# 64 tokens instead of 32 beside the gathered tile: 320 dense columns, rows from the queries on, row operands in PSUM, every second low part on GpSimd

## The chip, the core and the metric

One core of a Trainium2 chip runs the whole kernel. Its engines are TensorE (PE, matrix products into PSUM), VectorE (DVE), ScalarE (ACT), GpSimd (POOL, which also issues the gathers) and SyncE (SP, which issues the loads). The metric is the device time of one execution in microseconds.

## The reference

One layer on 512 tokens of width 2048, in float32: a mixer of two attentions, then a product-key expert layer, then a last RMSNorm. The change touches the expert layer alone:

```
def peer_ffn(h, w_query, sub_keys, expert_u, expert_v):
    q = (ht @ w_query).astype(jnp.float32).reshape(n_tok, PEER_HEADS, 2, HALF_KEY)
    scores = jnp.einsum('thpc,hpnc->thpn', q, sub_keys.astype(jnp.float32))
    s1, i1 = lax.top_k(scores[:, :, 0], PEER_TOPK)
    s2, i2 = lax.top_k(scores[:, :, 1], PEER_TOPK)
    ...
    top_score, pos = lax.top_k(cand_score, PEER_TOPK)
    expert_ids = jnp.take_along_axis(cand_id, pos, axis=-1)
    gates = jax.nn.softmax(top_score, axis=-1)
    ...
        u_sel = expert_u[idb]
        act = jax.nn.gelu(jnp.einsum('thkd,td->thk', u_sel, xb).astype(jnp.float32))
        w = (gb * act).astype(xb.dtype)
        v_sel = expert_v[idb]
        return jnp.einsum('thk,thkd->td', w, v_sel)
```

Each token picks 16 experts in each of 8 heads, 128 of 16384; an expert is one row of `expert_u` and one of `expert_v`, of 2048 numbers (8 KB) each.

## The kernel before

Activations lie with the feature dimension on partitions (`acc`: 16 tiles of 128 x 512 tokens). A product in float32 is made of three matmuls (`mm3`): `wload` loads a weight tile in two halves of 128 x 1024, ACT rounds each half to `wh` (the high part) and DVE subtracts to get `wl` (the low part); PE then multiplies wh by the two parts of the activation and wl by its high part. One `wload` feeds 48 matmuls. `wh` and `wl` have three buffers each, and the raw tiles four in all.

The expert layer is computed in two ways at once. For the first `TD` = 352 tokens (the dense ones) all 16384 experts are computed: `expert_up(c)` makes the activations of 128 experts with one wload of `uT` into the PSUM tile `psu`, and the products with `vP` go by groups of `GC` = 8 such chunks into `psy`, 16 output tiles to a group, each added to `acc` by DVE. The gates, zero for experts not chosen, are scattered through DRAM (`gsp`) and multiplied into the activations (`weigh`). The first `NS` = 54 activations are made before the gates are known and wait in DRAM (`gact_sp`, written and fetched again).

For the last 160 tokens the chosen rows are fetched. POOL issues an indirect DMA that brings 128 rows, one to each partition (`row_of`, a tile `row` of 128 x 2048). The last 128 tokens take one partition each and need 128 fetches from `expert_u` and 128 from `expert_v`. The `MB` = 32 tokens before them lie four times on the partitions (`GB` = 4 groups), so 32 fetches of each table (`SB`) serve them. For a row of `expert_u` one DVE operation multiplies it by the token's features `h2g` and sums up; for one of `expert_v` another adds it, times its weight, to the result. After the last one `back` and `back_b` transpose the results into `acc`.

The rows stand in a list `todo`. Each place in the code that calls `pace(ins, units)` adds `units * rate` to a counter; for each whole number reached, the next entry of the list is issued, its DVE work tied to come after `ins`. `rate` is `SLOW` = 0.8 until the down-projections begin, and then what spreads the rest evenly up to eight wloads before the end. Row buffers: two, and a third from the down-projections on. All engines run their instructions in the order that the framework's scheduler set.

Stages: attention and output projection; the queries (`psq2`, 16 wloads of `w_q`, per head the DVE chain `choose` for the gathered tokens); the choice for the dense tokens, woven with 40 early up-projections; the scatter of the gates with 14 more (`psgt`, `ab`); the down-projections, first with activations from DRAM, then alternating with the 74 up-projections that are left; the last norm.

Of the kernel before, what the change touches and what calls it, by code (L numbers as in the profile page):

```python
# [35 lines left out]
MB = 32  # L36
# [8 lines left out]
SLOW = 0.8  # L45
# [5 lines left out]
def block_kernel(ctx, tc, xT, gains, w_vf, bf, w_qk, w_v, w_g, w_br, w_o, w_q, keysT, uT, vP, expert_u, expert_v, outT):  # L51
# [43 lines left out]
    def wload(src, between=None, pace=None):  # L95
# [3 lines left out]
        for s in range(2):  # L99
# [9 lines left out]
            ins = nc.vector.tensor_tensor(lo, raw, hi.bitcast(F32), op=ALU.subtract)  # L109
            out.append((hi, lo))  # L110
            if pace and s == 0:
                pace(ins, 0.5)
# [378 lines left out]
    py = pool("py", 2, space=PSUM)  # L491
    gpool = pool("gath", 1)
    h2g = gpool.tile([P, KC, P], F32, name="h2g")
# [8 lines left out]
    rows_p = pool("rows", 1)  # L502
    accg = acc[:, :, T - P:]
    def norm2():
        ps = py.tile([P, T], F32, tag="py", name="psn2")
        nc.tensor.matmul(ps, ones, rstd, start=True, stop=True)
        rsqrt(rstd, ps, [gl.tile([P, T], F32, tag="gl", name="rs2") for i in range(3)])
        pt = py.tile([P, NT, P], F32, tag="py", name="psrt")
# [5 lines left out]
    def token_rows(cols, dst, x_dst=None):  # L514

        for j in range(0, KC, 4):
            if x_dst is not None:
                ps = py.tile([P, 4, P], F32, tag="py", name="psxg")
                for i in range(4):
                    nc.tensor.transpose(ps[:, i], cols(j + i), ident)  # L520
            ph = py.tile([P, 4, P], F32, tag="py", name="pshg")
            for i in range(4):
                tmp = gl.tile([P, P], F32, tag="gl", name="tmp")
                src = cols(j + i)
                nc.vector.tensor_scalar(tmp if len(src.shape) == 2 else tmp.rearrange("p (g m) -> p g m", m=MB), src,
                                        g_sb[:, KC + j + i:KC + j + i + 1], None, op0=ALU.mult)
# [19 lines left out]
    accb = h2g  # L546
    count, extra = [0], []
# [9 lines left out]
    def row_of(table, ids, i):  # L557
        count[0] += 1
        third = extra and count[0] % 3 == 0
        row = (extra[0] if third else rows_p).tile([P, KC, P], F32, tag="row", bufs=1 if third else 2, name="row")  # L560
# [4 lines left out]
    def gather_up(i, after):  # L565
        row = row_of(expert_u, idx, i)
        with tc.issue_after(after):
            nc.vector.scalar_tensor_tensor(row, row, rstd_t[:, NT - 1:NT], h2g, op0=ALU.mult, op1=ALU.mult,  # L568
                                           accum_out=gact[:, i:i + 1])

    def rows_b(i, after):
        token_rows(lambda k: acc[:, k, TD:TD + MB].unsqueeze(1).to_broadcast([P, GB, MB]), h2g)

    def gather_up_b(i, after):
        row = row_of(expert_u, idx_b, i)
        with tc.issue_after(after):
            nc.vector.scalar_tensor_tensor(row, row, rstd_b, h2g, op0=ALU.mult, op1=ALU.mult,
                                           accum_out=gact_b[:, i:i + 1])

    def gather_down(i, after):  # L580
# [3 lines left out]
        row = row_of(expert_v, idx, i)  # L584
        with tc.issue_after(after):
            nc.vector.scalar_tensor_tensor(accg, row, gact[:, i:i + 1], accg, op0=ALU.mult, op1=ALU.add)  # L586

    def gather_down_b(i, after):
# [3 lines left out]
        row = row_of(expert_v, idx_b, i)  # L592
        with tc.issue_after(after):
            if i == 0:
                nc.vector.tensor_scalar(accb, row, gact_b[:, :1], None, op0=ALU.mult)
            else:
                nc.vector.scalar_tensor_tensor(accb, row, gact_b[:, i:i + 1], accb, op0=ALU.mult, op1=ALU.add)

    def back(i, after):
        for j in range(0, KC, 4):  # L600
            ps = py.tile([P, 4, P], F32, tag="py", name="psback")
            for i in range(4):
                nc.tensor.transpose(ps[:, i], accg[:, j + i], ident)
            nc.scalar.activation(accg[:, j:j + 4], ps, AF.Copy)

    def back_b(i, after):
        for j in range(0, KC, 4):
            ps = py.tile([P, 4, MB], F32, tag="py", name="psbackb")
            for i in range(4):
                nc.tensor.matmul(ps[:, i], accb[:, j + i], sel_b, start=True, stop=True)  # L610
# [4 lines left out]
    todo += [(gather_down_b, i) for i in range(SB)] + [(lambda i, after: None, 0), (back, 0), (back_b, 0)]  # L615
    rate = [SLOW]

# [10 lines left out]
    with ExitStack() as s1:  # L628
# [3 lines left out]
        psx = pool("psx", 2, space=PSUM, cm=s1)  # L632
        pg = pool("pg", 2, space=PSUM, cm=s1)
# [82 lines left out]

        for h in range(NH):
            sc = []
            sv = se.tile([P, 2, HT, NK], F32, tag="sv", name="sv")
            for p in range(2):  # L720
# [3 lines left out]
                if b == 3:  # L724
                    token_rows(lambda k: acc[:, k, T - P:], h2g, accg)
                ps = pu.tile([P, T], F32, tag="pu", name="psq2")
                proj(ps, wload(w_q[b]), h2)
# [4 lines left out]
                ps = psx.tile([P, NT, NK], F32, tag="psx", name="pss")  # L732
# [16 lines left out]
        ps = psx.tile([P, T], F32, tag="psx", name="psrep")  # L749
# [177 lines left out]
```

## Time and profile before

| | |
|---|---|
| time, median of 3 runs | 3787.84 us (3779.3 to 3790.0) |
| the profiled execution, its own time | 3782.03 us |
| its span, first to last instruction | 3780.3 us |
| PE, DVE, ACT, POOL busy | 97%, 70%, 34%, 14% |
| DMA | 827.26 MB, mean 219 GB/s |
| mean granted PE clock | 0.989 |

Busy shares are means over all stages. A matmul's record overlaps the next one's, so what one matmul costs is read from the distance of two starts, not from its own length.

### The profile page before, as it was taken

What the parts mean: (1) busy time and instruction counts of PE and PEld (TensorE: products, weight loads), DVE (VectorE), ACT (ScalarE), POOL (GpSimd) and SP (SyncE); (2) the same over time, 40 slices, a digit from 0 to 9 for tenths busy, and PEclk for the clock granted to TensorE, in tenths of its full rate; (3) what the DMA queues carried; (4) which work ended last, traced back from release to release, by engine and by line L of the source; (5) the groups of instructions that cost most, each with busy time, mean ns of one, the idle gap of its engine ahead of it and who ended that gap; (6) DMA issues with size and microseconds to landing.
All of it is one profiled execution on the core that took longest, in us unless ns stands there. A gap on an engine that the chain in (4) does not pass through costs nothing.

```text
span 3780.3 us, 52236 instructions
## 1 busy us (share of the span) xinstructions
PE 3676.0 (97%) x20745; PEld 3384.4 (90%) x20745; DVE 2640.2 (70%) x4067; ACT 1291.3 (34%) x1808; POOL 515.2 (14%) x432
## 2 busy tenths in 40 slices
PE   8999999999999999999999898999999999999997
PEld 7888888888887878799999798999999999999997
DVE  5333445444555346799699888988888888888885
ACT  4334222232223223344355332333333333333333
POOL 0000000000000000011211122222222222222220
PEclk9999999999999999999999999999999999999999
DMA  4222222222224233376867899998999989999983
GB/s 141 80 78 77 98 95 95 89 87 84 85 95 138 95 100 101 128 267 251 294 229 264 288 336 333 352 334 326 333 336 348 345 324 349 340 343 344 332 306 112
DMA packets 233701, 827.26 MB, mean 219 GB/s; under 512 B 21736, under 2 KB 82664, under 8 KB 189680
## 3 DMA queue, kind: packets, MB, share of 16 engines
q1 hardware_dynamic: 174032, 450.30, 34.5%
q0 software_dynamic: 49920, 360.74, 24.8%
q10 hardware_dynamic: 9504, 12.88, 0.9%
q8 instruction: 163, 2.67, 0.3%
q14 instruction: 82, 0.67, 0.1%
HBM read 784.72 MB, written 39.11 MB: 218 GB/s over the span
## 4 chain that ended last, share of the span: by engine, by line
PE 81%; DVE 9%; DMA 5%; issue 3%; ACT 1%; SPq 0%; POOL 0%; DVEq 0%; POOLq 0%; ACTq 0%
PE psy L118 7%; PE psy L117 7%; PE psy L116 7%; PE psu L118 6%; PE psu L116 6%; PE psu L117 6%; PE psg L118 3%; PE psg L117 3%; PE psq L118 3%; PE psg L116 3%; PE psq L117 3%; PE psq L116 3%; DVE wl L109 2%; DVE ab L787 2%; PE psk L118 2%
## 5 line engine op out<-in xcount | busy, mean ns | idle before, releaser
L108 ACT ACTIVATE wh<-wr 128x1024 fp32r<-128x1024 f32 x768 | 813.6, 1061 | 1933.4 <-PE psy L117 581.0
L109 DVE TENSOR_TENSOR wl<-wr,wh 128x1024 fp32r<-128x1024 f32 x768 | 935.5, 1221 | 504.4 <-ACT wh L108 500.5
L116 PE MATMUL psy<-wg,wh 128*128 128x352 f32 x2048 | 668.6, 327 | 26.6 <-ACT wg L820 25.8
L117 PE MATMUL psy<-wg,wh 128*128 128x352 f32 x2048 | 672.0, 328 | 8.7 <-DVE wg L821 8.7
L118 PE MATMUL psu<-h,wl 128*128 128x352 f32 x2048 | 666.7, 326 | 12.8 <-DVE wl L109 12.5
L118 PE MATMUL psy<-wg,wl 128*128 128x352 f32 x2048 | 669.8, 328 | 8.4 <-DVE wl L109 8.3
L116 PE MATMUL psu<-h,wh 128*128 128x352 f32 x2048 | 666.6, 325 | 4.0 <-DVE gl L536 2.9
L117 PE MATMUL psu<-h,wh 128*128 128x352 f32 x2048 | 662.8, 324 | 0.0
L116 PEld LDWEIGHTS psy<-wg,wh 128*128 128x128 f32 x2048 | 391.1, 191 | 29.0 <-ACT wg L820 27.6
L118 PEld LDWEIGHTS psu<-h,wl 128*128 128x128 f32 x2048 | 385.5, 188 | 18.9 <-DVE wl L109 18.7
L117 PEld LDWEIGHTS psy<-wg,wh 128*128 128x128 f32 x2048 | 391.0, 191 | 11.0 <-DVE wg L821 10.9
L118 PEld LDWEIGHTS psy<-wg,wl 128*128 128x128 f32 x2048 | 391.0, 191 | 10.0 <-DVE wl L109 9.9
L116 PEld LDWEIGHTS psu<-h,wh 128*128 128x128 f32 x2048 | 386.6, 189 | 5.0 <-issue 3.2
L117 PEld LDWEIGHTS psu<-h,wh 128*128 128x128 f32 x2048 | 386.9, 189 | 0.0
L561 POOL DMA_INDIRECT row<-eu,idx x128 | 192.4, 1503 | 901.5 <-DVE row L568 606.4
L568 DVE SCALAR_TENSOR_TENSOR row<-row,rstd_t,h2g 128x2048 f32<-128x2048 f32 x128 | 300.1, 2345 | 6.5 <-DMA row<-eu,idx 6.5
L586 DVE SCALAR_TENSOR_TENSOR acc<-row,gact,acc 128x2048 f32<-128x2048 f32 x128 | 300.1, 2345 | 1.9 <-DMA row<-ev,idx 1.9
L561 POOL DMA_INDIRECT row<-ev,idx x128 | 182.2, 1424 | 508.0 <-DVE acc L586 478.1
L116 PE MATMUL psq<-h,wh 128*128 128x512 f32 x512 | 204.5, 399 | 8.8 <-ACT wh L108 8.8
L117 PE MATMUL psq<-h,wh 128*128 128x512 f32 x512 | 205.6, 401 | 1.5 <-DVE h L167 1.4
L118 PE MATMUL psq<-h,wl 128*128 128x512 f32 x512 | 204.6, 400 | 0.1
L118 PE MATMUL psg<-h,wl 128*128 128x512 f32 x512 | 203.3, 397 | 0.0
(311 smaller groups left out, 5513.7 us busy)
## 6 DMA issues: line engine op xcount, KB each, us to landing
wr<-uT SPq DMA_DIRECT2D x256, 512.0 KB
wr<-vP SPq DMA_DIRECT2D x256, 512.0 KB
wr<-w_qk SPq DMA_DIRECT2D x64, 512.0 KB
wr<-w_g SPq DMA_DIRECT2D x64, 512.0 KB
gsp<-st POOLq DMA_DIRECT2D x22, 1024.0 KB
wr<-w_br SPq DMA_DIRECT2D x32, 512.0 KB
wr<-w_o SPq DMA_DIRECT2D x32, 512.0 KB
wr<-w_q SPq DMA_DIRECT2D x32, 512.0 KB
```

The lines of the kernel that those rows point to most:

```text
L108: nc.scalar.activation(hi, raw, AF.Copy)
L109: ins = nc.vector.tensor_tensor(lo, raw, hi.bitcast(F32), op=ALU.subtract)
L116: nc.tensor.matmul(ps, wh, ah, start=start, stop=False)
L117: nc.tensor.matmul(ps, wh, al, start=False, stop=False)
L118: nc.tensor.matmul(ps, wl, ah, start=False, stop=stop)
L561: nc.gpsimd.indirect_dma_start(out=row.rearrange("p k q -> p (k q)"), out_offset=None, in_=table, in_offset=bass.IndirectOffsetOnAxis(ap=i ...
L568: nc.vector.scalar_tensor_tensor(row, row, rstd_t[:, NT - 1:NT], h2g, op0=ALU.mult, op1=ALU.mult, accum_out=gact[:, i:i + 1])
L586: nc.vector.scalar_tensor_tensor(accg, row, gact[:, i:i + 1], accg, op0=ALU.mult, op1=ALU.add)
L787: nc.vector.tensor_scalar(ab[0][:, i], i128, tr[0][:, t:t + 1], tr[2][:, t:t + 1], op0=ALU.is_equal, op1=ALU.mult)
```

## The change

- `MB` goes from 32 to 64: 192 tokens are gathered, in the 128 of the full tile and two groups of 64 (`GB` = 2), with `SB` = 64 fetches of each table for the latter; 320 tokens stay dense, and 53 up-projections come early.
- Gathers of the full tile start in the queries' stage: after each head its part of `idx` is computed, and `qpace` takes rows that are known (`QROWS` = 0.75 times 2 units a wload, from the sixth wload on). `SLOW` becomes 1.1.
- The features that the rows are multiplied by, and the sums of the down rows, lie in PSUM (`hold`, four banks) instead of SBUF; the sums are copied to SBUF once (`sums`) before they are transposed. `back` comes right after the last row of the full tile and adds to `acc`. There are three row buffers throughout. The other PSUM pools shrink to two banks for `psu` and two shared by everything else (`px`, also `psy`, which had four).
- From the queries on, the second half's low part in each wload is computed on POOL, not on DVE.
- The gates of the next group are fetched while the present one is multiplied (`gates`), and its first activation is weighed two wloads before the group ends.

```diff
-MB = 32
+MB = 64
...
-SLOW = 0.8
+SLOW = 1.1
+QROWS = 0.75
...
-            ins = nc.vector.tensor_tensor(lo, raw, hi.bitcast(F32), op=ALU.subtract)
+            second = more and s == 1
+            ins = (nc.gpsimd if second else nc.vector).tensor_tensor(lo, raw, hi.bitcast(F32), op=ALU.subtract)
...
-    py = pool("py", 2, space=PSUM)
+    px = pool("px", 2, space=PSUM)
+    pr = pool("pr", 1, space=PSUM)
...
-    rows_p = pool("rows", 1)
-    accg = acc[:, :, T - P:]
+    rows_p = pool("rows", 3)
+    held = [None]
+
+    def hold(name):
+
+        held[0] = pr.tile([P, KC, P], F32, tag="pr", name=name)
+        return held[0]
...
-            nc.vector.scalar_tensor_tensor(row, row, rstd_t[:, NT - 1:NT], h2g, op0=ALU.mult, op1=ALU.mult,
+            nc.vector.scalar_tensor_tensor(row, row, rstd_t[:, NT - 1:NT], held[0], op0=ALU.mult, op1=ALU.mult,
                                            accum_out=gact[:, i:i + 1])
...
+    def add_row(row, g, i, ins):
+        with tc.issue_after(ins):
+            if i == 0:
+                nc.vector.tensor_scalar(hold("accg"), row, g[:, :1], None, op0=ALU.mult)
+            else:
+                nc.vector.scalar_tensor_tensor(held[0], row, g[:, i:i + 1], held[0], op0=ALU.mult, op1=ALU.add)
...
+        def qpace(after, units):
+
+            if HK - len([f for f, _ in todo if f is gather_up]) < known[0]:
+                pace(after, units)
...
-                proj(ps, wload(w_q[b]), h2)
+                proj(ps, wload(w_q[b], pace=qpace if b > 4 else None, units=2.0), h2)
...
+            nc.vector.scalar_tensor_tensor(idx[:, hk], ia[:, NT - 1, hk], float(NK), ib[:, NT - 1, hk], op0=ALU.mult,
+                                           op1=ALU.add)
+            known[0] += TOPK
...
             w = wload(vP[grp, jb])
+            if grp + 1 < NG and jb == 1:
+                gates(grp + 1)
+            if grp + 1 < NG and jb == KC // JJ - 2:
+                first.append(weigh((grp + 1) * GC))
             for jj in range(JJ):
                 j = jb * JJ + jj
-                ps = (py, py2)[j % 2].tile([P, T], F32, tag="py", name="psy")
+                ps = px.tile([P, T], F32, tag="px", name="psy")
```

How the order on two engines changes shows in three places. On POOL, all of the `expert_v` fetches for the full tile follow each other in the kernel before (`row` is the fetched tile, `ev` the table):

```order
L561 DMA row<-eu,idx 128x2048 x83
L561 DMA row<-eu,idx_b 128x2048 x32
L561 DMA row<-ev,idx 128x2048 x128
L561 DMA row<-ev,idx_b 128x2048 x32
L874 TENSOR_TENSOR acc<-acc,rstd 128x512 x4
```

In the changed kernel, in the middle of the `expert_v` fetches, low parts stand between them:

```order
L558 DMA row<-ev,idx 128x2048 x2
L111 TENSOR_TENSOR wl<-wr,wh 128x1024
L558 DMA row<-ev,idx 128x2048
L111 TENSOR_TENSOR wl<-wr,wh 128x1024
L558 DMA row<-ev,idx 128x2048 x2
L111 TENSOR_TENSOR wl<-wr,wh 128x1024
```

One or two fetches now stand behind each low part, and each low part behind the fetches before it.

On DVE, at the start of a block of up-projections in the late part, the kernel before has (`gl<-psu,rstd` takes a finished product, `gl<-gl,h_8494` multiplies by the gates):

```order
L536 TENSOR_TENSOR gl<-psu,rstd 128x352
L586 SCALAR_TENSOR_TENSOR acc<-row,gact,acc 128x16x128
L817 TENSOR_TENSOR gl<-gl,h_8494 128x352
L586 SCALAR_TENSOR_TENSOR acc<-row,gact,acc 128x16x128
L821 TENSOR_TENSOR wg<-gl,wg 128x352
L109 TENSOR_TENSOR wl<-wr,wh 128x1024 x2
```

and the changed one, near the end of the rows:

```order
L537 TENSOR_TENSOR gl<-psu,rstd 128x320
L582 SCALAR_TENSOR_TENSOR accg<-row,gact_b,accg 128x2048
L830 TENSOR_TENSOR gl<-gl,h_8494 128x320
L582 SCALAR_TENSOR_TENSOR accg<-row,gact_b,accg 128x2048
L834 TENSOR_TENSOR wg<-gl,wg 128x320
L111 TENSOR_TENSOR wl<-wr,wh 128x1024
```

One low part of the two has gone to POOL, the 352 columns are 320, and the sum `accg` is the tile in PSUM.

On DVE in the queries' stage, between the instructions of `choose`, the changed kernel has row operations, which the kernel before has only after that stage:

```order
L648 MAX v<-pss 128x8
L565 SCALAR_TENSOR_TENSOR row,gact<-row,rstd_t,h2g 128x2048
L649 MAX_INDEX i<-v,pss 128x8
L650 MATCH_REPLACE tk<-v,pss 128x128
L648 MAX v<-pss 128x8
L651 MAX v<-tk 128x8
L649 MAX_INDEX i<-v,pss 128x8
L652 MAX_INDEX i<-v,tk 128x8
L650 MATCH_REPLACE tk<-v,pss 128x128
L565 SCALAR_TENSOR_TENSOR row,gact<-row,rstd_t,h2g 128x2048
```

Sixteen of the 384 row operations stand in this stage, and about 75 before the down-projections begin (43 of 320 in the kernel before).

## Rows read from the trace of the kernel before

**Rows 1.** The page: engines' busy time; DMA share in 40 slices, in tenths.

```profile
PE 3676.0 (97%) x20745; PEld 3384.4 (90%) x20745; DVE 2640.2 (70%) x4067; ACT 1291.3 (34%) x1808; POOL 515.2 (14%) x432
...
DMA  4222222222224233376867899998999989999983
```

**Rows 2.** Windows by stage: length; PE, PEld, DVE, ACT, POOL busy; clock; DMA share, GB/s.

```profile
1372.00:1590.00 218.00, 214.40 (x1006) 174.25 (x1007) 151.15 (x637) 76.36 (x169) 0.18 (x1) 0.98 0.33 107
1590.00:1910.00 320.00, 308.13 (x1875) 304.02 (x1874) 276.07 (x734) 140.74 (x228) 49.48 (x34) 0.98 0.74 266
1910.00:2130.00 220.00, 194.63 (x1364) 187.41 (x1362) 208.39 (x508) 123.59 (x131) 28.33 (x35) 0.97 0.72 259
2130.00:2567.00 437.00, 412.58 (x2449) 407.59 (x2450) 378.44 (x456) 132.43 (x159) 111.92 (x73) 0.96 0.92 334
2567.00:3692.00 1125.00, 1116.40 (x6896) 1112.96 (x6896) 960.87 (x909) 369.65 (x438) 290.13 (x201) 1.00 0.90 334
3692.00:3780.00 88.00, 69.26 (x429) 67.31 (x427) 46.77 (x70) 29.55 (x40) 4.94 (x4) 0.91 0.32 113
```

**Rows 3.** Windows of 512 columns and of two blocks; timeline of 264 columns.

```profile
1220.00:1360.00 140.00, 140.00 (x605) 113.83 (x604) 54.06 (x61) 40.12 (x49) 0.00 (x0) 1.00 0.28 96
...
3445.70:3507.90 62.20, 62.20 (x386) 62.20 (x385) 54.66 (x48) 18.00 (x18) 19.98 (x12) 1.00 0.95 353
3507.90:3569.60 61.70, 61.70 (x386) 61.70 (x385) 52.76 (x49) 23.04 (x30) 13.08 (x12) 1.00 0.89 338
...
48.09 0.28 PE L232 MATMUL psvf<-wh,h 128*128 128x264 f32 x1
...
51.99 0.28 PE L234 MATMUL psvf<-wh,h 128*128 128x264 f32 x1
```

**Rows 4.** Groups by line, late part, 2567 to 3692 us: busy, mean, idle before.

```profile
L109 DVE TENSOR_TENSOR wl<-wr,wh 128x1024 fp32r<-128x1024 f32 x286 | 347.7, 1219 | 22.7 <-ACT wh L108 20.7 <-issue 0.8
...
L586 DVE SCALAR_TENSOR_TENSOR acc<-row,gact,acc 128x2048 f32<-128x2048 f32 x128 | 300.1, 2345 | 1.9 <-DMA row<-ev,idx 1.9
...
L561 POOL DMA_INDIRECT row<-ev,idx x128 | 182.2, 1424 | 508.0 <-DVE acc L586 478.1 <-DMA row<-ev,idx 12.0 <-DVE acc L841 9.3
L577 DVE SCALAR_TENSOR_TENSOR row<-row,rstd_b,h2g 128x2048 f32<-128x2048 f32 x32 | 74.9, 2344 | 6.8 <-DMA row<-eu,idx_b 6.8
...
L597 DVE SCALAR_TENSOR_TENSOR h2g<-row,gact_b,h2g 128x2048 f32<-128x2048 f32 x31 | 72.7, 2344 | 0.0
...
L817 DVE TENSOR_TENSOR gl<-gl,h 128x352 f32<-128x352 f32 x71 | 36.8, 518 | 38.2 <-DMA h<-gsp 38.2
...
L568 DVE SCALAR_TENSOR_TENSOR row<-row,rstd_t,h2g 128x2048 f32<-128x2048 f32 x12 | 28.1, 2345 | 0.0
```

**Rows 5.** Windows of 20 us where the DMA engines are fullest.

```profile
2420.00:2440.00 20.00, 19.61 (x121) 19.21 (x120) 19.47 (x24) 5.82 (x6) 5.99 (x4) 1.00 1.00 381
...
3200.00:3220.00 20.00, 20.00 (x125) 20.00 (x124) 18.69 (x18) 6.36 (x7) 7.29 (x5) 1.00 1.03 381
```

**Rows 6.** Groups of instructions by line, tail (from 3692 us).

```profile
L876 DVE SCALAR_TENSOR_TENSOR acc<-acc,g_sb,psr 128x512 f32<-128x512 f32 x12 | 8.0, 739 | 2.8 <-ACT rstd L871 2.8
L874 POOL TENSOR_TENSOR acc<-acc,rstd 128x512 f32<-128x512 f32 x4 | 4.9, 1261 | 102.7 <-ACT rstd L871 102.7
```

**Rows 7.** Groups on DVE by line, scatter (1910 to 2130 us).

```profile
L787 DVE TENSOR_SCALAR ab<-i,ia,gt 128x128 f32<-128x128 f32 x352 | 97.7, 343 | 0.0
L782 DVE TENSOR_TENSOR ab<-i,ib 128x512 f32<-128x512 f32 x88 | 60.2, 684 | 0.0
L109 DVE TENSOR_TENSOR wl<-wr,wh 128x1024 fp32r<-128x1024 f32 x29 | 35.0, 1216 | 0.0
```

**Rows 8.** The chain that ended last, 2530 to 2560 us: start, us, what.

```profile
2537.84 1.68 POOL row L561
...
2541.71 7.99 DMA row<-eu,idx
...
2549.72 2.36 DVE row L568 x2
```

More of the change, by code (lines that the diff above doesn't have):

```diff
@@ L93, in block_kernel, with wload @@
     WC = D // 2 + 4 * NH
-    def wload(src, between=None, pace=None):
+    def wload(src, between=None, pace=None, units=0.5):
         out = []
@@ L557, in row_of @@
     def row_of(table, ids, i):
[L558 to L560 removed]
+        row = rows_p.tile([P, KC, P], F32, tag="row", name="row")
         nc.gpsimd.indirect_dma_start(out=row.rearrange("p k q -> p (k q)"), out_offset=None, in_=table,
@@ L583, in gather_down @@
             nc.vector.tensor_tensor(gact, gact, ggate, op=ALU.mult)
-        row = row_of(expert_v, idx, i)
-        with tc.issue_after(after):
-            nc.vector.scalar_tensor_tensor(accg, row, gact[:, i:i + 1], accg, op0=ALU.mult, op1=ALU.add)
+        add_row(row_of(expert_v, idx, i), gact, i, after)
     def gather_down_b(i, after):
@@ L614, in block_kernel @@
     todo += [(gather_up_b, i) for i in range(SB)] + [(gather_down, i) for i in range(HK)]
-    todo += [(gather_down_b, i) for i in range(SB)] + [(lambda i, after: None, 0), (back, 0), (back_b, 0)]
-    rate = [SLOW]
+    todo += [(back, 0)] + [(gather_down_b, i) for i in range(SB)] + [(back_b, 0)]
+    rate = [QROWS]
     gact_sp = dram.tile([NS, P, TD], F32, name="gact_sp")
@@ L803, in fetch, with gates @@
         return g
+    def gates(grp):
+        for b in range(0, TD // TB, 8):
+            e = min(b + 8, TD // TB)
+            nc.sync.dma_start(gg[:, b:e], gsp[:, b:e, grp * GC:(grp + 1) * GC])
     ahead = []
@@ L811, in weigh @@
             ahead.append(fetch(len(ahead)))
-        if n % GC == 0:
-            for b in range(0, TD // TB, 8):
-                e = min(b + 8, TD // TB)
-                nc.sync.dma_start(gg[:, b:e], gsp[:, b:e, n:n + GC])
         g = ahead[n]
@@ L822, in weigh @@
         return wg
+    gates(0)
     ws = [weigh(0)]
@@ L826, in block_kernel @@
     rate[0] = len(todo) / (2 * NK - NS - 8)
-    py2 = pool("py2", 2, space=PSUM)
     for grp in range(NG):
+        first = []
         while len(ws) < GC:
@@ L842, in block_kernel @@
                 pace(add, 1.0 / JJ)
-        ws = []
+        ws = first
     while todo:
         pace(add, 1.0)
-    fin = [rows_p.tile([P, 4, T], F32, tag="row", bufs=2, name="fin") for i in range(2)]
+    fin = [rows_p.tile([P, 4, T], F32, tag="row", name="fin") for i in range(2)]
     ssq = fin[0][:, 0]
```

79 lines of the change are left out of this document (35 added, 44 removed).

## The prediction

> **What bounds the kernel now.** I read the page first, then the stages, then the groups of the last stage. The page shows TensorE (PE) busy for 97% of the span [rows 1]. That figure alone proves little, since matmuls are pipelined. The stages say more: in each, look at which engine is nearly full and what the DMA engines move [rows 2]. Up to 1372 us (attention and output projection) nothing changes, and I leave that part out. Then come the queries (1372 to 1590), the choice of experts woven with 40 up-projections (to 1910), the scatter of the gates with 14 more (to 2130), the first down-projections, whose activations come back from DRAM (to 2567), and a late part of alternating down- and up-projections (to 3692). A tail of 88 us ends it.
>
> The late part is PE's own pace. Its unit is a block of eight weight loads, each load 48 matmuls, so 384 matmuls. Two neighbouring blocks take 62.2 and 61.7 us with PE busy all the time and the clock at 1.00, the higher of its levels, 2.4 GHz [rows 3]. That is 61.7/384 = 161 ns a matmul of 352 columns. The whole part, 143 loads (286 halves of `wl`, [rows 4]) in 1125 us, comes to 7.87 us a load or 62.9 us a block, so boundaries between groups cost little. But two others stand close behind: DMA at share 0.90 and 334 GB/s, and VectorE (DVE) at 961 of 1125 us. In the scatter DVE is the fuller one: 208 of 220 us [rows 2].
>
> **What a narrower matmul gives.** The trace has three widths. 512 columns: 605 matmuls in 140 us, 231.4 ns [rows 3]. 264 columns: from 48.09 to 51.99 us are 32 steps, 121.9 ns. The slope is 109.5/248 = 0.44 ns a column; it puts 352 at 160.8, where 161 is seen, so 320 columns lie on the same line at 147 ns. 12288 matmuls become 352 to 320 wide (2048 in each of six groups), which is 12288 x 14 = 172 us. That is the most the change can take from PE's work. A block's floor falls to 384 x 147 = 56.4 us.
>
> **What it adds.** Sixty-four more rows of 128 x 2048 f32, 1.049 MB each (32 up, 32 down): 67 MB. In the new order 306 rows fall to the last 24 blocks, 12.75 a block, where the trace has 204 rows on 143 loads, 11.4 a block [rows 4]. A block then moves 16 halves of 0.524 MB (8.39 MB), 12.75 rows (13.37) and half a group's gates (0.66): 22.4 MB. At PE's floor that asks for 397 GB/s. The blocks of before had 353 at share 0.95, which is 372 at a full share [rows 3]; the best 20 us have 381 at shares of 1.00 and 1.03 [rows 5]. So the DMA engines become the late part's limit. I take 370 GB/s: the block's own rate at a full share, since in the two best stretches buffers had just come free. Bounds: 344, the mean of the two blocks, and 397, the floor of PE. A block: 60.5 us (56.4 to 65.1). PE will idle between loads, and where it does so now its clock is granted at 0.96 to 0.98 on average [rows 2]; in a part that DMA paces, that slowness fills time that is idle anyway.
>
> DVE in a block of up-projections loses eight low parts of 1.22 us and gets 1.35 rows of 2.35 more. With 320 columns the 0.52 us operations shrink to about 0.48: 8 x 1.22 + 24 x 0.48 + 12.75 x 2.35 = 51 us of 60.5. It is no limit by itself. The row operand in PSUM I cost at nothing: the 512-wide operation of this kind that reads PSUM takes 739 ns [rows 6], 1.44 ns an element with its fixed part, and the SBUF row takes 1.15 over four times the length. Nothing in the trace reads and writes 2048 columns in PSUM; 10% more on the 384 rows would be 90 us of DVE, and lies under its 16% of room.
>
> GpSimd (POOL) gets 272 low parts. The nearest row is its 128x512 product at 1261 ns [rows 6], so 2.5 us for 1024 columns (at least 1.26). A block is 8 x 2.5 + 12.75 x 1.42 = 38 us of 60.5. They lie behind PE's work as long as they come a load ahead. The matmuls that read them wait only if the queue is late. Queued behind each is the next row's DMA issue, and the DVE operation on that row waits for it.
>
> **The sum, stage by stage.**
> - Queries: 16 rows now fall here, 38 us of DVE against 67 us of room (151 of 218 busy), and 16 low parts leave DVE (20 us). Hidden, but with rows that must land in an in-order queue: +3 (0 to +10).
> - Choice: 40 loads x 48 x 14 ns = 27 us less PE work, of which DVE, 276 of 320 us busy, lets most through: -18 (-27 to 0).
> - Scatter: DVE sets it. Two of 22 token blocks go (158 us of `ab`, -14, [rows 7]), 16 of 29 low parts (-19), four rows come (+9): 208 becomes 184. The low parts on POOL and the wait for the gates at the end give some back: -10 (-20 to 0).
> - First down-projections: 51 loads, 79 rows, 8.7 MB of activations (one load's is 164 KB), 9.2 MB of gates: 154 MB, 417 us at 370 GB/s, 437 now: -20 (-45 to +10).
> - Late part: 17.9 blocks x 60.5 = 1083 us against 1125: -42 (-115 to +40).
> - Tail: 8.5 loads x 0.67 us without rows: -6.
>
> That is -93. The profiled execution took 3782.03 us, 1.7 more than its span of 3780.3, and becomes 3689. It lies 5.8 us under the median of 3787.84, so I predict **3695 us**.
>
> The rest costs nothing: 16 transposes and 4 copies fewer in the queries, the gates of a group fetched a group ahead (that takes away waits such as DVE's 38.2 us for `gsp`, most of which PE didn't feel [rows 4]), and `psy` in two PSUM banks instead of four. That last one hides only while DVE takes each sum within one matmul group, 24 x 147 ns = 3.5 us; a late row there stops PE at once.
>
> **Rivals.** The measurement tells about 0.3% from no change, 11 us.
>
> *The row loop, slower.* Three row buffers; each goes through issue (1.68 us), landing, DVE (2.35) and perhaps a low part on POOL ahead of the next issue (2.5 us in 8 of 12.75 cases, 1.6 on average). A row that DVE waited for landed 10.2 us after its issue [rows 8]. With that each time the cycle is 15.8 us, 5.27 a row, and a block 67.2: late part +77, the others -50 or so, hence about 3815. From a landing of 9.2 us on (14.8/3 = 4.93 us a row, 62.9 a block) the late part gains nothing. Against it: in the late part DVE idled for rows only 1.9 us on 128 rows and 6.8 on 32 [rows 4]. Chance 0.15.
>
> *PE sets the pace throughout.* The DMA engines give 397 GB/s: late -115, first down-projections -45, the others as above: 3595 us, or up to 3640 with some waits left. The 381 of single stretches speak for it, the two blocks against it. Chance 0.12.
>
> *DVE and POOL take turns.* If a low part on POOL and a DVE operation with two SBUF inputs exclude each other, 24 such operations in an up-projection block (`wl`, `gl` times gate, `wg`) meet a busy POOL one time in three, 1.25 us each: 10 us, and 51 becomes 61. With waits of POOL in return I put 63 us on half the blocks, and nothing gained in choice and scatter: 9 x 2.5 + 28 = 51 us given back, 3745. The Trainium skill (SBUF — State Buffer, Who interferes with whom) says that a VectorE instruction with two SBUF inputs contends with a GpSimd instruction that reads SBUF and that one of them blocks for the whole instruction. No run here shows it: before, POOL computes nothing beside DVE in these stages. Chance 0.15.
>
> *The change buys nothing.* If 344 GB/s is all that weights and rows together get, a block takes 65.1 us, the late part loses 40 and the first down-projections 11, where the other stages gain 31: 3808. At 350 GB/s it is 3781; in between there is no difference to be told. The 20 us at 381 speak against it. The Trainium skill (SBUF — State Buffer, A bandwidth-pool intuition that's wrong) puts HBM at about 358 GB/s a core; as an estimate by that page a block takes 62.6 us and the total is 3745; the stretches at 381 disagree with it. Chance 0.13.
>
> **How the numbers follow.** My forecast has 0.45, with its own range of 3660 to 3735. Faster by over 0.3%: 0.45 + 0.12 + 0.15 = 0.72. Within: 0.13. Slower: 0.15, the row loop. The range runs from 3620 (half of the PE-paced cases left out, 0.06) to 3800 (the row loop left out, 0.15): 0.79.
>
> **What would show it.** Right: PE's matmuls 147 ns apart inside a load, blocks of 59 to 62 us, DMA share at 0.95 or more with about 370 GB/s, PE idle a few us a block for `wl`, `wg` or a PSUM bank, DVE waiting for `row` from DMA. Wrong: matmuls still 155 ns or more apart; DVE's row operation off 2.35 us; POOL's low part over 3 us, or DVE's `wl` above 1.22 us, which would be the exclusion; DMA share falling below 0.9 while DVE waits for rows, which would be the row loop.

## The result

The changed kernel takes 3836.25 us (median of 4 runs, 3833.08 to 3845.54) where the kernel before takes 3787.38 beside it: ratio 1.0137 [1.0113, 1.0160], 49 us slower, where I had forecast 3695. The profiled execution took 3835.57 us with a span of 3833.9, and its mean granted clock fell from 0.989 to 0.968.

The page of the changed kernel, first the engines (answers to [rows 1]), then two groups of low parts (columns: busy, mean of one | idle before):

```profile
PE 3555.4 (93%) x20665; PEld 3242.6 (85%) x20665; DVE 2650.1 (69%) x3856; ACT 1274.8 (33%) x1798; POOL 1168.8 (30%) x766
...
L111 DVE TENSOR_TENSOR wl<-wr,wh 128x1024 fp32r<-128x1024 f32 x496 | 622.4, 1255 | 457.6 <-ACT wh L109 455.4
L111 POOL TENSOR_TENSOR wl<-wr,wh 128x1024 fp32r<-128x1024 f32 x272 | 658.8, 2422 | 447.9 <-ACT wh L109 348.2
```

POOL does its 272 low parts at 2.42 us each, as I had put it (2.5). But PE, which has 172 us less to do, is busy only 121 us less: it waits more, and its clock is lower.

The stages of the changed kernel as windows (choice, scatter, first down-projections, late part, tail; columns as in [rows 2]). The cuts here and below are each kernel's own events: first up-projection, first scatter product, first down product, first up-projection after the down-projections began, last one.

```profile
1580.00:1925.00 345.00, 302.75 (x1960) 296.74 (x1959) 306.62 (x778) 153.31 (x249) 155.48 (x83) 0.93 0.77 279
1925.00:2152.00 227.00, 181.24 (x1247) 172.44 (x1247) 208.45 (x457) 113.45 (x121) 58.62 (x48) 0.91 0.67 244
2152.00:2572.00 420.00, 366.10 (x2323) 356.05 (x2324) 336.34 (x408) 121.77 (x149) 213.26 (x122) 0.94 0.91 337
2572.00:3751.00 1179.00, 1077.54 (x7075) 1060.34 (x7073) 966.93 (x804) 373.30 (x452) 627.03 (x380) 0.97 0.93 350
3751.00:3834.00 83.00, 63.32 (x426) 61.29 (x424) 48.64 (x63) 29.68 (x40) 23.14 (x12) 0.89 0.35 121
```

The first four of the kernel before, cut at the same events (its tail has 89 us):

```profile
1577.00:1910.00 333.00, 321.11 (x1956) 316.62 (x1955) 286.74 (x797) 146.50 (x243) 49.48 (x34) 0.98 0.73 259
1910.00:2129.00 219.00, 194.63 (x1364) 187.41 (x1362) 207.44 (x505) 123.20 (x130) 28.33 (x35) 0.98 0.72 260
2129.00:2541.00 412.00, 387.57 (x2296) 383.17 (x2297) 356.00 (x428) 124.00 (x148) 105.70 (x68) 0.96 0.91 333
2541.00:3691.00 1150.00, 1140.40 (x7043) 1136.38 (x7042) 984.26 (x939) 378.47 (x450) 296.36 (x206) 1.00 0.90 334
```

So these four stages each became longer: +12, +8, +8 and +29. In each, PE idles more (length less busy: 42, 46, 54 and 101 us, where before had 12, 24, 24 and 10) and the clock is down. The late part moves 350 GB/s at share 0.93, not the 370 forecast.

PE's waits from 1580 to 3751 us, by what ended them (total, times, longest, in us):

```profile
PE psu L120 <- DVE wl L111: 91.0, 48, 5.0
PE psy L118 <- ACT wg L833: 38.1, 6, 11.8
PE psgt L803 <- DVE ab L801: 28.5, 19, 2.5
PE psy L118 <- DVE acc L859: 24.7, 13, 5.5
PE psy L120 <- DVE wl L111: 15.7, 10, 3.9
```

The whole list adds up to 243 us, 186 of them for VectorE; that of the kernel before, over the same stages, to 70, 7.3 of them for `ab` and for `wl`:

```profile
PE psu L118 <- DVE wl L109: 12.5, 15, 2.6
```

PE waits above all for the half of the low parts that VectorE kept; no wait for GpSimd's own low parts is in the list. Why VectorE is late is seen in the groups on DVE, from 1580 to 3750 us:

```profile
L111 DVE TENSOR_TENSOR wl<-wr,wh 128x1024 fp32r<-128x1024 f32 x248 | 317.8, 1282 | 26.4 <-ACT wh L109 26.4
L582 DVE SCALAR_TENSOR_TENSOR accg<-row,gact,accg 128x2048 f32<-128x2048 f32 x127 | 298.0, 2347 | 27.3 <-DMA row<-ev,idx 27.0
...
L834 DVE TENSOR_TENSOR wg<-gl,wg 128x320 fp32r<-128x320 f32 x127 | 145.1, 1155 | 12.3 <-ACT wg L833 11.9
...
L801 DVE TENSOR_SCALAR ab<-i,ia,gt 128x128 f32<-128x128 f32 x320 | 112.9, 415 | 0.0
L830 DVE TENSOR_TENSOR gl<-gl,h 128x320 f32<-128x320 f32 x127 | 93.3, 745 | 100.1 <-DMA h<-gsp 53.5 <-DMA gl<-gact_sp 40.8 <-ACT gl L540 5.5
L537 DVE TENSOR_TENSOR gl<-psu,rstd 128x320 f32<-128x320 f32 x127 | 61.1, 481 | 83.2 <-PE psu L120 82.9
```

Instructions take longer than their columns ask. L537 is the measure: two inputs of 320 columns, one of them in PSUM, 481 ns. `wg` and `gl` times `h`, of the same width with both inputs in SBUF, take 1155 and 745; the latter took 518 at 352 columns [rows 4]. `ab` took 343 ns [rows 7] and now 415. The row operation with its PSUM operand stays at 2347 (2336 to 2356 over all 127). One place shows what happens (timeline: start, us, what; VectorE, then GpSimd, then PE's next matmuls):

```profile
3242.45 2.35 DVE L582 SCALAR_TENSOR_TENSOR accg<-row,gact,accg 128x2048 f32<-128x2048 f32 x1
3244.71 2.12 DVE L834 TENSOR_TENSOR wg<-gl,wg 128x320 fp32r<-128x320 f32 x1
3246.75 1.21 DVE L111 TENSOR_TENSOR wl<-wr,wh 128x1024 fp32r<-128x1024 f32 x1
...
3244.12 2.35 POOL L111 TENSOR_TENSOR wl<-wr,wh 128x1024 fp32r<-128x1024 f32 x1 [3.25 <-ACT wh L109]
...
3248.01 0.41 PE L120 MATMUL psy<-wg,wl 128*128 128x320 f32 x1 [3.92 <-DVE wl L111]
...
3249.80 0.47 PE L118 MATMUL psy<-wg,wh 128*128 128x320 f32 x1
...
3252.47 0.42 PE L119 MATMUL psy<-wg,wh 128*128 128x320 f32 x1
3252.72 0.31 PE L120 MATMUL psy<-wg,wl 128*128 128x320 f32 x1
...
3253.90 0.31 PE L119 MATMUL psy<-wg,wh 128*128 128x320 f32 x1
```

GpSimd's low part runs from 3244.12 to 3246.47. VectorE's `wg`, started inside it, ends only after it, at 3246.83: 1.64 us more than its usual 0.48. The low part behind it on VectorE is late by that much. PE stands 3.92 us for it: 1.64 of them are the hold, the other 2.28 come from VectorE's own order, a row and `wg` ahead of the low part. What follows is the second cost: from 3249.80 to 3252.47 ten steps, 267 ns each; then eight steps from 3252.72 to 3253.90, 147 ns. The windows of that place name it (columns as before):

```profile
3245.90:3249.30 3.40, 1.29 (x9) 1.29 (x10) 3.40 (x4) 0.75 (x2) 1.61 (x2) 1.00 1.07 355
3249.30:3252.70 3.40, 3.40 (x14) 3.40 (x14) 2.45 (x2) 0.00 (x0) 1.67 (x1) 0.50 1.13 368
3252.70:3256.10 3.40, 3.40 (x24) 3.40 (x24) 2.75 (x2) 1.06 (x1) 1.98 (x1) 1.00 1.04 372
```

After a stretch in which PE mostly stood, the granted clock is 0.50 (1.2 GHz), and PE does 14 matmuls where it then does 24: ten fewer, 1.5 us of work. Over the run, (1 - 0.968) x 3833.9 is 123 us of clock by this estimate, against (1 - 0.989) x 3780.3, 42 us, before.

### The profile page after: what moved, and what is told of

It is laid out like the page before. It is cut to its first block, busy times and chain, and to the rows that moved or that the text cites. A ratio compares the mean times of both kernels' runs of the same rounds, so it can differ in the third digit from the quotient of the medians.

```text
span 3833.9 us, 52828 instructions
## 1 busy us (share of the span) xinstructions
PE 3555.4 (93%) x20665; PEld 3242.6 (85%) x20665; DVE 2650.1 (69%) x3856; ACT 1274.8 (33%) x1798; POOL 1168.8 (30%) x766
## 4 chain that ended last, share of the span: by engine, by line
PE 61%; DVE 18%; DMA 12%; issue 4%; ACT 2%; POOL 1%; SPq 1%; DVEq 0%; POOLq 0%; ACTq 0%
PE psy L118 5%; PE psy L119 4%; PE psy L120 4%; PE psg L120 3%; PE psg L119 3%; PE psg L118 3%; PE psq L120 3%; PE psq L119 3%; PE psu L120 3%; PE psq L118 3%; DVE wl L111 3%; PE psu L118 3%; PE psu L119 3%; DVE row L565 2%; DMA h<-gsp 2%
## 5 line engine op out<-in xcount | busy, mean ns | idle before, releaser
L111 DVE TENSOR_TENSOR wl<-wr,wh 128x1024 fp32r<-128x1024 f32 x496 | 622.4, 1255 | 457.6 <-ACT wh L109 455.4
L111 POOL TENSOR_TENSOR wl<-wr,wh 128x1024 fp32r<-128x1024 f32 x272 | 658.8, 2422 | 447.9 <-ACT wh L109 348.2
L120 PE MATMUL psu<-h,wl 128*128 128x320 f32 x2048 | 645.8, 316 | 91.2 <-DVE wl L111 91.0
L118 PE MATMUL psy<-wg,wh 128*128 128x320 f32 x2048 | 647.1, 317 | 73.3 <-ACT wg L833 38.1
L120 PE MATMUL psy<-wg,wl 128*128 128x320 f32 x2048 | 645.4, 315 | 15.7 <-DVE wl L111 15.7
L119 PE MATMUL psy<-wg,wh 128*128 128x320 f32 x2048 | 647.0, 316 | 12.3 <-DVE wg L834 12.3
L118 PE MATMUL psu<-h,wh 128*128 128x320 f32 x2048 | 645.8, 315 | 12.5 <-DVE gl L537 7.0
L119 PE MATMUL psu<-h,wh 128*128 128x320 f32 x2048 | 643.3, 314 | 0.0
L118 PEld LDWEIGHTS psu<-h,wh 128*128 128x128 f32 x2048 | 395.0, 193 | 18.5 <-ACT wh L109 12.1
L119 PEld LDWEIGHTS psu<-h,wh 128*128 128x128 f32 x2048 | 395.0, 193 | 0.0
L582 DVE SCALAR_TENSOR_TENSOR accg<-row,gact,accg 128x2048 f32<-128x2048 f32 x127 | 298.0, 2347 | 27.3 <-DMA row<-ev,idx 27.0
L558 POOL DMA_INDIRECT row<-eu,idx x128 | 159.1, 1243 | 320.2 <-DVE row L565 165.6
L558 POOL DMA_INDIRECT row<-ev,idx x128 | 148.7, 1162 | 209.1 <-DVE accg L582 181.7
```

The source lines that it names most:

```text
L111: ins = (nc.gpsimd if second else nc.vector).tensor_tensor(lo, raw, hi.bitcast(F32), op=ALU.subtract)
L118: nc.tensor.matmul(ps, wh, ah, start=start, stop=False)
L119: nc.tensor.matmul(ps, wh, al, start=False, stop=False)
L120: nc.tensor.matmul(ps, wl, ah, start=False, stop=stop)
L558: nc.gpsimd.indirect_dma_start(out=row.rearrange("p k q -> p (k q)"), out_offset=None, in_=table, in_offset=bass.IndirectOffsetOnAxis(ap=i ...
L582: nc.vector.scalar_tensor_tensor(held[0], row, g[:, i:i + 1], held[0], op0=ALU.mult, op1=ALU.add)
```

## The experiments

**Theory A** is the rival "DVE and POOL take turns": GpSimd's low part holds VectorE's operations for its length, VectorE's own low part comes late, PE stands, and its clock drops. **Theory Q**, its main rival, is the row loop: low parts stand in POOL's queue ahead of the rows' issues, three row buffers don't cover it, and the DMA engines run short. A third possibility is that 64 tokens in two groups (the slot groups below) and the narrower columns buy nothing whatever POOL does. Each ratio below is to the kernel before. Runs 9 and 10 are edits of the kernel before, all others of the changed one.

**1, thin: GpSimd computes 128 of the low part's 1024 columns.**

```diff
-            ins = (nc.gpsimd if second else nc.vector).tensor_tensor(lo, raw, hi.bitcast(F32), op=ALU.subtract)
+            if second:
+                nc.gpsimd.tensor_tensor(lo[:, :P], raw[:, :P], hi[:, :P].bitcast(F32), op=ALU.subtract)
+                lo = lo[:, :P]
...
```

(The products with this half then read these 128 columns for every block.)

> The changed kernel, but GpSimd computes only the first 128 of the 1024 columns of its low part, and all eight matmul blocks of that half read these 128 columns (so the products of that half's low part are not the reference's). Order, buffers and waits stay; GpSimd's operation shrinks from 2.4 us to about 0.4. Theory A (exclusion: a GpSimd operation that reads SBUF holds back VectorE operations with two SBUF inputs, 210 us of lengthened VectorE operations in the changed kernel): these operations return to their usual length, PE's waits for low parts and weights fall by more than half, 3690 to 3745 us. Theory B (rows and DMA engines: 67 MB more and three row buffers set the pace, wherever the low parts are made): 3810 to 3840 us, PE's waits stay.

3717.36 us, 0.9823 [0.9804, 0.9841]: 119 us less than the changed kernel. Its groups on DVE, choice to late part:

```profile
L587 DVE SCALAR_TENSOR_TENSOR accg<-row,gact,accg 128x2048 f32<-128x2048 f32 x127 | 298.4, 2350 | 25.0 <-DMA row<-ev,idx 24.6 <-DVE gl L542 0.4
...
L835 DVE TENSOR_TENSOR gl<-gl,h 128x320 f32<-128x320 f32 x128 | 64.2, 513 | 126.3 <-DMA gl<-gact_sp 60.0 <-DMA h<-gsp 47.2 <-ACT gl L545 19.0
L839 DVE TENSOR_TENSOR wg<-gl,wg 128x320 fp32r<-128x320 f32 x128 | 63.8, 512 | 7.5 <-ACT wg L838 7.2
```

and its stages, choice to late part:

```profile
1577.00:1886.00 309.00, 294.00 (x1961) 290.54 (x1960) 266.39 (x778) 154.10 (x249) 78.36 (x83) 0.97 0.84 310
1886.00:2091.00 205.00, 175.80 (x1248) 167.01 (x1246) 187.06 (x457) 113.10 (x122) 34.13 (x48) 0.96 0.73 269
2091.00:2496.00 405.00, 359.92 (x2323) 351.61 (x2322) 313.34 (x407) 121.11 (x147) 115.71 (x122) 0.95 0.92 349
2496.00:3623.00 1127.00, 1065.41 (x7070) 1051.64 (x7069) 872.88 (x803) 370.95 (x451) 339.99 (x380) 0.98 0.96 367
```

All four stages gain: 36, 22, 15 and 52 us against the changed kernel. `wg` and `gl` are back near 0.5 us. The late part is now what the prediction had drawn: 367 GB/s at share 0.96. Of the 141 us between forecast and result, 119 are the low part on GpSimd. VectorE waits as long for these rows as in the changed kernel (24.6 against 27.0 us), but now it is busy for 873 of 1127 us, where it was for 967 of 1179.

**2, writes: as 1, and GpSimd fills the other 896 columns twice, reading nothing.**

```diff
+                for i in range(2):
+                    nc.gpsimd.memset(lo[:, P:].bitcast(F32), 0.0)
```

> As the kernel with 128 columns, but GpSimd also fills the other 896 columns with zeros, twice (writes only, reading nothing), so that it is about as busy as in the changed kernel. Theory A with reads as the cause: VectorE's operations keep their usual length, and the time is that of the kernel with 128 columns within 20 us (3690 to 3760). If it is GpSimd's queue (its time, the gathers standing behind it): near the changed kernel, 3800 to 3850. Theory B: 3810 to 3840.

3776.94 us, 0.9984 [0.9969, 0.9999], above what was expected. The choice is as short as in 1 (309 us) and the scatter takes 215, so work that only writes costs much less there. But the late part takes 1181 us, as long as in the changed kernel, although VectorE isn't held (first line, choice to late part). The group on POOL, over the whole run, says why it may:

```profile
L839 DVE TENSOR_TENSOR wg<-gl,wg 128x320 fp32r<-128x320 f32 x126 | 61.1, 499 | 15.0 <-ACT wg L838 14.8
...
L114 POOL MEMSET wl<- 128x896 f32 x544 | 463.3, 853 | 319.3 <-PE psy L125 179.0 <-PE psu L125 97.7 <-PE psq L125 37.0
```

The fills wait 314 us for PE, whose matmuls have to free the buffer of `wl`, and the rows' issues stand behind them. So reading and writing are told apart in what they do to VectorE; in the late part the time is lost all the same, without a hold.

**3, split4: the low part on GpSimd in four operations of 256 columns.**

```diff
+                for q in range(0, n, n // 4):
+                    nc.gpsimd.tensor_tensor(lo[:, q:q + n // 4], raw[:, q:q + n // 4],
+                                            hi[:, q:q + n // 4].bitcast(F32), op=ALU.subtract)
```

> The changed kernel with GpSimd's low part in four operations of 256 columns (about 0.65 us each) instead of one of 1024. Theory A: VectorE is held for at most one piece at a time, so its lengthened operations sum to about a third of 210 us: 3760 to 3805 us. Theory B or a busy GpSimd queue: 3836 us or somewhat more, from the fixed part of three more operations.

3824.76 us, 1.0099 [1.0080, 1.0117], within little of the changed kernel and above the expectation. VectorE is busy 2558 us, 92 less than in the changed kernel and nearly half of the way to run 1 (2455), but the time falls by 12 us of 119: it doesn't follow the hold alone. The group shows the catch:

```profile
L113 POOL TENSOR_TENSOR wl<-wr,wh 128x256 fp32r<-128x256 f32 x1088 | 846.2, 810 | 409.9 <-ACT wh L109 317.0 <-DMA h<-gsp 58.1 <-ACT f L672 14.5
```

Four quarters take 3.2 us where the whole took 2.4. Shorter holds, more of them: the choice gains 16 us, the late part none (1178).

**4, dvelow: all low parts on VectorE again, the rest as changed** (`ins = nc.vector.tensor_tensor(lo, raw, ...)`).

> The changed kernel with all low parts on VectorE again (that part of the change undone). Theory A: nothing is lengthened any more, but VectorE gets 272 x 1.22 = 332 us of work; an up-projection block has 51 + 9.8 = 61 us of it, so 3770 to 3830 us with PE waiting for a busy VectorE. Theory B: 3836 us or more, since nothing about rows changes.

3804.34 us, 1.0055 [1.0037, 1.0073]. Choice 327 and scatter 209 us are better than with GpSimd's help. The late part (1185) is not: DVE is busy 1031 of it, and from the choice to its end PE waits 115 us for VectorE's low parts. With GpSimd out of the way VectorE's own work makes them late.

**5, rows4: a fourth row buffer from the down-projections on** (in a pool that is free by then).

```diff
+        count[0] += 1
+        fourth = extra and count[0] % 4 == 0
+        row = (extra[0] if fourth else rows_p).tile([P, KC, P], F32, tag="row", bufs=1 if fourth else 3, name="row")
```

> The changed kernel with a fourth row buffer from the down-projections on. Theory Q (in the late part the loss comes from gathers that stand in GpSimd's queue behind low parts, so that three buffers don't cover the landing): the fourth buffer covers it, the late part falls from 1179 us to 1140 or less, the total to 3800 or less. Theory D (the DMA engines have no more to give, or VectorE is held whatever is prefetched): the late part stays within 12 us, 3825 to 3845.

3802.24 us, 1.0046 [1.0030, 1.0063]: 34 us less than the changed kernel. The late part falls from 1179 to 1141 us, while its DMA rises from 350 to 361 GB/s; choice and scatter stay long (344 and 231). On DVE, from 1578 to 3715 us:

```profile
L585 DVE SCALAR_TENSOR_TENSOR accg<-row,gact,accg 128x2048 f32<-128x2048 f32 x127 | 297.8, 2345 | 0.0
...
L838 DVE TENSOR_TENSOR wg<-gl,wg 128x320 fp32r<-128x320 f32 x127 | 144.2, 1148 | 14.6 <-ACT wg L837 14.3
```

VectorE is held as before (1148 ns for 1155), but no longer waits for these rows. So in the late part the loss goes for the most part through rows that come late, as theory Q has it; whether they are late by POOL's queue or by the hold, this run doesn't say.

**6, thin with half of the slot-group rows: as 1, 64 rows fewer, their terms missing from the sums.**

```diff
-    todo += [(gather_up_b, i) for i in range(SB)] + [(gather_down, i) for i in range(HK)]
+    todo += [(gather_up_b, i) for i in range(0, SB, 2)] + [(gather_down, i) for i in range(HK)]
```

(`gather_down_b` likewise.)

> The kernel with GpSimd's low part of 128 columns, and every second row of the two slot groups left out (64 of 384 rows, as many as the change added; the sums of those rows are missing). If the DMA engines set the late part's pace in the kernel with 128 columns (1127 us at share 0.96): with 14% fewer bytes PE does, 147 loads at 7.06 us and some waits, 1050 to 1080 us, total 3625 to 3670. If VectorE, the PSUM banks or the row loop do: the late part stays above 1110, total 3690 or more.

3637.45 us, 0.9615 [0.9590, 0.9641]. The late part (cut 5 us ahead of its events):

```profile
2480.00:3553.00 1073.00, 1046.82 (x7098) 1038.86 (x7098) 763.66 (x741) 371.56 (x456) 286.51 (x332) 0.99 0.91 337
```

With less to move PE is busy 1047 of 1073 us; its floor is 147 loads x 48 x 147 ns = 1037. So in 1 the added rows set the late part, and not PE or its PSUM banks. The share of 0.96 there speaks for the DMA engines; but this run also takes row operations from VectorE (764 us busy for 873) and turns from the row loop, and doesn't tell these apart.

**7, busy: as 1, and four fills of a scratch tile that nobody reads, behind each thin low part.**

```diff
+                with tc.issue_after(low.ins):
+                    for i in range(4):
+                        nc.gpsimd.memset(scratch, 0.0)
```

> The kernel with 128 columns, and behind each of these operations four fills of a tile of 448 columns that nobody reads, so that GpSimd is busy some 2 us more a load without reading SBUF and without waiting for a buffer. If GpSimd's time in its queue costs the late part (gathers come later): 1160 us or more there, total 3760 to 3785. If the kernel with writes lost its time because its fills wait for buffers that PE holds: late part 1125 to 1145, total 3715 to 3740. In the choice and the scatter both expect no loss against the kernel with 128 columns (309 and 205 us), since nothing is read.

3716.59 us, 0.9816 [0.9800, 0.9833], the time of 1, with a GpSimd as busy as in the changed kernel (1168.8):

```profile
PE 3530.3 (95%) x20665; PEld 3227.6 (87%) x20665; DVE 2458.1 (66%) x3856; ACT 1274.1 (34%) x1798; POOL 1147.3 (31%) x1854
```

The choice takes 309 us again. Fills that read nothing and wait for no buffer cost nothing that the medians show. (The late part takes 1142 us in the profiled execution, which lies 12 us above the median.)

**8, mb32: the changed kernel with `MB = 32` and all low parts on VectorE.**

> The rest of the change alone: MB = 32 again (352 dense columns, 320 rows), all low parts on VectorE; rows from the queries on, row operands and sums in PSUM, three row buffers throughout, two PSUM banks for the sums, gates fetched ahead. If these parts are worth something by themselves (group boundaries, an earlier start of rows): 3750 to 3780 us. If two banks or rows among the queries cost: 3795 or more.

3785.34 us, 0.9993 [0.9983, 1.0003], between the two expectations: the order of rows, PSUM operands, three row buffers, two banks for the sums and early gates together buy nothing at 32 tokens.

**9, before with POOL's low parts alone** (the one line of the change in the kernel before).

> The kernel before with one part of the change alone: every second low part from the queries on is made by GpSimd. Its row operations still have two SBUF inputs. Theory A (exclusion): they are now held as well, 320 of them at 2.35 us, and hold GpSimd in return; lengthened VectorE operations sum to 300 us or more, the total is 3830 us or more, although VectorE has 332 us less work. Without exclusion: VectorE is relieved in choice and scatter, 3740 to 3785 us.

3918.59 us, 1.0358 [1.0340, 1.0375]. This one line makes the kernel before 133 us slower than its runs beside it (3785.9). Here the row operation has two SBUF inputs, and it is held too (groups on DVE; [rows 4] had 2345 for both):

```profile
L569 DVE SCALAR_TENSOR_TENSOR row<-row,rstd_t,h2g 128x2048 f32<-128x2048 f32 x128 | 406.9, 3179 | 3.3 <-DMA row<-eu,idx 3.3
L587 DVE SCALAR_TENSOR_TENSOR acc<-row,gact,acc 128x2048 f32<-128x2048 f32 x128 | 368.0, 2875 | 3.4 <-DMA row<-ev,idx 3.2
```

The timeline of two such meetings (VectorE's lines, then GpSimd's):

```profile
2600.24 4.60 DVE L569 SCALAR_TENSOR_TENSOR row<-row,rstd_t,h2g 128x2048 f32<-128x2048 f32 x1
...
2626.90 2.34 DVE L569 SCALAR_TENSOR_TENSOR row<-row,rstd_t,h2g 128x2048 f32<-128x2048 f32 x1
...
2600.28 2.40 POOL L110 TENSOR_TENSOR wl<-wr,wh 128x1024 fp32r<-128x1024 f32 x1
...
2627.02 4.46 POOL L110 TENSOR_TENSOR wl<-wr,wh 128x1024 fp32r<-128x1024 f32 x1 [0.80 <-issue]
```

Two operations of 2.35 and 2.40 us that meet take 4.60 and 2.40, or 2.34 and 4.46: one keeps its length, and the other's grows by nearly all of it. In the first, VectorE's record starts 0.04 us before GpSimd's and VectorE is held all the same.

**10, before with `MB = 64` alone.**

> The kernel before with MB = 64 alone: 320 dense columns, 384 rows, all low parts on VectorE, row operands in SBUF. Nothing excludes anything; VectorE has 61 us of work for an up-projection block of 60: near the changed kernel with all low parts on VectorE (ratio 1.0055), 3780 to 3830 us. If the 64 tokens are a gain by themselves that GpSimd's part took away: 3750 or less.

3867.91 us, 1.0205 [1.0178, 1.0232], above the expectation. The late part takes 1252 us with DVE busy 1088 of it. More rows on two or three buffers and a VectorE that still makes every low part is a loss; against run 4, which has the PSUM operands, buffers and order of the change as well, it is 64 us worse. So these together do help at 64 tokens, and run 8 says not at 32.

**11 and 12: the changed kernel with four row buffers as in 5, and GpSimd's low parts only from the down-projections on (11), or only in the loads of down-projections themselves (12).** The edit of 12 (in 11 a flag, set where the down-projections begin, takes the place of `down`):

```diff
-            second = more and s == 1
+            second = down and s == 1
...
-            w = wload(vP[grp, jb])
+            w = wload(vP[grp, jb], down=True)
```

> The changed kernel with four row buffers from the down-projections on, and GpSimd's low parts only from there on (VectorE makes them in queries, choice and scatter). Stages as measured apart: choice 327, scatter 209 (all low parts on VectorE), first down-projections 420 and late part 1141 (four buffers), tail 84: 3760 us. If the stages act on each other (the choice on VectorE leaves a backlog): 3780 or more.

> The changed kernel with four row buffers, and GpSimd's low parts only in the loads of down-projections, where VectorE has one operation with two SBUF inputs a load in the late part (three in up-projections). Theory A: little is held in the late part, but an up-projection block has 61 us of VectorE work again; late part 1130 to 1160, total 3750 to 3780 us. If what is held did not matter there: late part 1165 or more, because VectorE is full.

Run 11 takes 3772.33 us, 0.9962 [0.9950, 0.9974], between its two expectations: its choice, scatter and first down-projections are as added up (326, 213 and 420 us), its late part is 1149 for 1141. Run 12 takes 3748.63, 0.9904 [0.9886, 0.9923]. Both are faster than either kernel. The late part of 12:

```profile
2535.00:3663.00 1128.00, 1071.20 (x7086) 1051.59 (x7085) 978.44 (x877) 373.62 (x452) 495.38 (x305) 0.98 0.95 365
```

1128 us at 365 GB/s is as short as in 1, with the low parts computed in full. I put them there because VectorE's work beside a down-projection is sums into `acc` and rows, each with one operand in PSUM. The mean of `wg` in this run is 667 ns, against 1155 in the changed kernel: fewer meetings, not none.

## Why the prediction was wrong

**The step that failed** is "They lie behind PE's work as long as they come a load ahead": GpSimd's low parts at no cost in the sum. The operation was sized right (2.42 for 2.5 us), and PE never waits for its result; but it costs 119 us (3836 - 3717, run 1), against a whole forecast gain of 93. The sum had looked at who waits for the result, and not at what the operation does to VectorE while it runs, and it priced the rows' issues queued behind it at nothing. From the DVE groups above: `wg` 127 x (1155 - 480), `gl` 127 x (745 - 480), `ab` 320 x (415 - 343) and `wl` 248 x (1282 - 1219) ns are 86 + 34 + 23 + 16, some 158 us added to an in-order engine on which PE waits.

**The rival that came true** is "DVE and POOL take turns", at 0.15 and with 51 us given back. That they exclude each other is shown (runs 1 and 9, and the meetings in the timelines), and that it is the reading, not a busy GpSimd, is shown in the choice, where runs 2 and 7 lose nothing (309 us). What the rival put on VectorE was right for the late part: 10 us in a block of up-projections, where `wg` 78 x (1512 - 524), `gl` 74 x (738 - 499) and `wl` 147 x (1238 - 1223) ns against run 1 are 97 us on the 9.4 blocks that its 75 up-projections make, some 10 each. The groups of `wg` in the late part, the changed kernel's and run 1's:

```profile
L834 DVE TENSOR_TENSOR wg<-gl,wg 128x320 fp32r<-128x320 f32 x78 | 117.8, 1512 | 10.3 <-ACT wg L833 10.3
...
L839 DVE TENSOR_TENSOR wg<-gl,wg 128x320 fp32r<-128x320 f32 x78 | 40.7, 524 | 5.4 <-ACT wg L838 5.4
```

Too small by more than half was what followed from it. I had read 61 us of work in a block of 60.5 as 2.5 us lost. But PE stops for a late low part while VectorE still has room (busy 967 of 1179 us). Against run 1 the late part lost 52 us where I had 22.5 (9 x 2.5), choice and scatter 58 where I had 28, the first down-projections 15 where I had none.

The low clock I had put at nothing, as it "fills time that is idle anyway" in a part that the DMA engines pace; at 350 GB/s they didn't. For the same 20665 matmuls PE is busy 3555.4 us in the changed kernel and 3520.4 in the profiled execution of run 1 (`PE 3520.4 (95%)`, span 3706.2): 35 us more of slower matmuls, and the rest of the spans' difference of 128 us, 93, is PE idling. The granted clock gives about as much, 123 - 82 = 41 us ((1 - 0.978) x 3706.2 for run 1), and the lists of waits 243 - 150 = 93. What the 35 us would have cost by themselves isn't shown: no run has changed the clock alone.

The rule of the Trainium skill that I weighed (SBUF — State Buffer, Who interferes with whom) holds here in the parts that a run shows: two SBUF inputs on VectorE against a GpSimd instruction that reads SBUF, one of them blocked for the whole instruction (4.60 for 2.35 us, 4.46 for 2.40), and no contention where VectorE has one input in SBUF and the other in PSUM (2347 ns). The trace of before had no row to confirm it; the rule should have had more than 0.15 all the same.

**The row loop**, the rival of the slower side, was real in the late part: a fourth buffer brought 38 of 52 us back there (run 5), with VectorE held as much as before, and run 2 lost 54 us there against run 1 with VectorE not held. So the hold is shown as the cause in the choice; in the late part the loss goes through late rows for the greater part, and the hold is one of the things that may make them late. The rival's price of 77 us by landings of 10.2 us [rows 8] was not what decided, as the other stages lost without it. I had put the loop at nothing in the sum because VectorE hardly waited for rows before (1.9 and 6.8 us [rows 4]); that trace had no low parts in POOL's queue. What makes the loop long, VectorE's held operations or the low parts ahead of the issues, isn't told apart: run 3 shortens the one and lengthens the other and leaves the late part as it was, run 7 has the busy queue without a loss in the medians, run 2 the waiting queue with one.

**What was right.** The matmul of 320 columns is 147 ns. The row operand in PSUM is 2.35 us, so nothing, and more than that: in run 9, without it, POOL's low parts hold the rows too. Queries +3 (1577 to 1580 us). With GpSimd nearly out of the way most of the forecast stands: run 1 has 3717 against 3695, its late part 367 GB/s against my 370, and run 6 agrees with the DMA engines as the limit there without proving it. Against the kernel before, run 1 gives choice -24 (forecast -18), scatter -14 (-10), first down-projections -7 (-20), late part -23 (-42) and tail -6 (-6). The down-projections were over-counted: in the first of them the DMA reaches 349 GB/s, and from the choice to the late part PE still waits 39.7 us for `wg` and, as I had feared for two banks of `psy`, 26.0 us for `acc`.

"The change buys nothing" (a DMA ceiling of 344 to 350) was wrong as a mechanism, although the late part did run at 350: that was no ceiling, since run 1 moves the same 413 MB at 367. (The mean of the two blocks that I gave as 344 is 345.5: 353 and 338.)

**What stays open:** why the late part of run 2 loses all that run 1 had gained; what makes the rows late in the late part of the changed kernel; what the slower clock costs by itself; whether the DMA engines or the row loop limit run 1; and whether a better place than run 12's exists: its choice (326 us) and scatter (212) are still 17 and 7 us longer than in run 1, with VectorE making all low parts there, and its `wg` and `gl` still take 667 and 664 ns.

## What to carry to other kernels

Work moved from a busy VectorE to an idle GpSimd isn't free for VectorE: look up which VectorE instructions with two SBUF inputs run beside it, and charge each meeting with up to the other's whole length. Put such work where VectorE's second operands lie in PSUM. Don't ask only whether VectorE has room for what is added: ask what waits for the results behind it. Behind a wait of PE of a few microseconds, look for matmuls at half the clock and count them too. And when an in-order queue that issues transfers gets other work, try one more buffer before judging the change.

## What the runs showed that was not expected

- GpSimd's subtraction takes 2422 ns for 1024 columns, 810 for 256 and 503 for 128 (means, with what VectorE held it): cutting it in four cost a third more (run 3).
- VectorE's `ab`, with one tensor and two columns of scalars as inputs, is held as well (343 to 415 ns), and so it is beside fills that only write (419 ns in run 2, 385 in run 7, where run 1 without the fills has 352); `wg` isn't (499 and 514 ns).
- 367 GB/s held for 1127 us (run 1), and 365 in run 12.
